# Weight splits behind the reading of each attention projection, and group 0's scaling taken out of the merge

## The chip, the core and the metric

The kernel runs on one core of a Trainium2 chip. The metric is the device time of one execution in microseconds (us). Engines are named as in the profile: PE (matmuls), PEld (its weight loads), DVE (vector), ACT (scalar), POOL (GpSimd) and SP (which only issues DMAs here).

## The reference, cut to what matters

One inference step of a two-layer decoder for 512 prompt positions and 8 sample sequences of 8 positions, all in float32. Layer 0 mixes positions by attention and a pooling mixer, layer 1 by a short convolution; a gated feed-forward half-step stands before and behind each mixer. The attention has 8 heads and three dilation groups, whose outputs are merged with weights from their softmax denominators:

```python
for g, (win, dil) in enumerate(DIL_PATTERNS):      # (128,1), (512,4), (2048,16)
    q, k, v = qk[:, :, g, 0], qk[:, :, g, 1], qkv[:, :, g, 2]     # q, k after rotary
    ...
    o, lse = dilated_attn_prompt(q, k, v, dil)     # or dilated_attn_sample with the cache
    outs.append(o); lses.append(lse)
wts = jax.nn.softmax(jnp.stack(lses, axis=0), axis=0)[..., None]
a = jnp.sum(wts * jnp.stack(outs, axis=0), axis=0)
```

## The kernel before

All 576 tokens lie on the free axis. Each float32 product is made of three matmuls with rounded parts: a weight unit comes by one DMA of 1 MB into `raw` (two buffers), and each half of it is split into a high part `wh` (an ACT cast) and the rest `wl` (a DVE subtraction), line 100 and 101, with three buffers of each. `Weights.next(ahead)` first emits the splits up to `ahead` halves beyond the one that is used now. The split of a unit's second half is followed at once by the DMA of the unit after next into the freed `raw` buffer, on SP's queue, which also carries the loads of the cached keys and values.

The attention loop (lines 1081 to 1114) runs over four pairs of heads. For each it makes six projections (48 matmuls each): q and k of group 1, of group 2 and of group 0. Between the projections stands the rest of the work of the pair of heads before: scores of group 0 (P0), the sample scores, the merge, the transposes of the scaled probabilities and the products with the values. The order is written out by hand and kept: each engine takes its instructions in program order. What sets the pace beside that is PSUM: projections, scores, transposes and products share four buffers named `acc`, used in turn, so each new one waits until the one four places earlier has been read.

`rotate` makes a projection and reads it on DVE: a product with the rotary table (line 1291) and a shuffle (line 1292). POOL then multiplies the shuffled copy (line 1293) and forms q (lines 1311 and 1312) or k (lines 1322 and 1325). `merge` works out the group weights (`mw`, ending in line 1396) and scales the probabilities: P1 on ACT (line 1403), P2 on DVE (line 1405), the first half of P0 on DVE (line 1409) and the second on POOL (lines 1411 and 1414). `sample_weights` (lines 1504 to 1508) scales the sample probabilities on DVE; `sample_pv` ends in the copy `So` out of PSUM (line 1536); `transposes` (line 1427) end in copies `PT` (lines 1430 and 1434). After the loop the last pair's rest stands among four projections for the pooling mixer, which call `proj` directly.

Of the kernel before, what the change touches and what calls it, by code (L numbers as in the profile page):

```python
# [34 lines left out]
KD = 8  # L35
# [132 lines left out]
def ch(t):  # L168

    return t.rearrange("p (c n) -> p c n", c=2)  # L170


class Trunk:
# [216 lines left out]
        self.turn(outs, f, toks)  # L390


    def part(self, p, rh, rl, k0, kn, first, last, mid={}):
        nc = self.nc
        h, l = self.W.next()
        for k in range(kn):
            wh = h[:, k * 128:k * 128 + 128]
            wl = l[:, k * 128:k * 128 + 128]
            for z, (w, m) in enumerate(((wh, rh), (wh, rl), (wl, rh))):
                for c in range(2):  # L400
                    nc.tensor.matmul(out=p[:, c, :C], lhsT=w, rhs=m[:, k0 + k, c * C:c * C + C],  # L401
                                     start=(first and k == 0 and z == 0), stop=(last and k == kn - 1 and z == 2))
            if k in mid:
                mid[k]()

    def proj(self, rh, rl, mid={}):
        p = self.acc()
        self.part(p, rh, rl, 0, KD, True, True, mid)
        return p


# [617 lines left out]
class Mixer:  # L1029
# [5 lines left out]
    def run(self, nxt, u0):  # L1035
        t, nc, I = self.t, self.nc, self.I
        with ExitStack() as ctx:
# [42 lines left out]
            prev = None  # L1080
            for hp in range(4):
                cur = {"hp": hp, "U": self.tile("U", [128, 2, 3, 2, 8], bufs=2), "ks": self.tile("ks", [128, 4, 64], bufs=2),
                       "q": {}, "k": {}, "P": {}, "PT": {}, "qbd": self.qbd[hp % 2], "S": {}, "N": {}, "ST": {}, "SN": {}, "so": {}}
                self.q(cur, 1)
                if prev:
                    self.scores0(prev)
                    self.sample_scores(prev, 0)
                    self.exchange(prev)
                    self.sample_weights(prev, 0)
                self.k(cur, 1)  # L1090
                if prev:
                    self.sample_transposes(prev, 0)
                    self.sample_scores(prev, 1)
                    self.merge(prev)
                    self.sample_weights(prev, 1)
                self.q(cur, 2)
                if prev:
                    self.sample_pv(prev, 0)
                    self.transposes(prev, (1, 2, (0, 0)))
                self.scores12(cur, 1)  # L1100
                self.k(cur, 2)
                if prev:
                    self.pv(prev)
                    self.sample_transposes(prev, 1)
                    self.sample_out(prev, 0)
                self.q(cur, 0)
                self.scores12(cur, 2)
                if prev:
                    self.sample_pv(prev, 1)
                self.k(cur, 0)  # L1110
                if prev:
                    self.sample_out(prev, 1)
                self.new_keys(cur, 0)
                prev = cur
# [8 lines left out]
            self.sample_transposes(prev, 0)  # L1123
            self.sample_scores(prev, 1)
            self.merge(prev)
            self.sample_weights(prev, 1)
            self.pool_in(pu, 2)
            self.pool_diff(3)
# [37 lines left out]
            for e, d in enumerate(ORDER):  # L1166
                p = t.proj(t.xh, t.xl)
# [116 lines left out]

    def rotate(self):
        t, nc = self.t, self.nc
        p = t.proj(t.xh, t.xl)
        self.flush()
        a = self.tile("rot", [128, 720], bufs=4)[:, :NT]
        b = self.tile("rot", [128, 720], bufs=4)[:, :NT]  # L1290
        nc.vector.tensor_tensor(out=ch(a), in0=p[:, :, :C], in1=ch(self.rope[:, 0, :]), op=ALU.mult)
        nc.vector.stream_shuffle(ch(b), p[:, :, :C], SWAP16)
        nc.gpsimd.tensor_tensor(out=b, in0=b, in1=self.rope[:, 1, :], op=ALU.mult)
        return a, b

# [48 lines left out]
    def scores12(self, s, g):  # L1344
        nc, t = self.nc, self.t
        p = t.acc()
        P = s["P"][g] = self.tile(f"P{g}", [128, 2, 4, 128])
        for h in range(2):
# [3 lines left out]
        for h in range(2):  # L1352
            for r in range(4):
                self.softmax_rows(s, g, 2 * r + h, p[:, h, 128 * r:128 * r + 128], self.m1 if g == 1 else self.m2, P[:, h, r, :])

    def scores0(self, s):
        nc, t = self.nc, self.t
        P = s["P"][0] = self.tile("P0", [128, 2, 4, 256])
        for h in range(2):
# [6 lines left out]
            for i in range(4):  # L1366
                lo = 128 if i == 0 else 0
                self.softmax_rows(s, 0, 2 * i + h, p[:, i // 2, (i % 2) * 256 + lo:(i % 2) * 256 + 256], self.m0[:, lo:], P[:, h, i, lo:])

# [9 lines left out]
    def merge(self, s):  # L1379

        nc, U = self.nc, s["U"]
        m = self.tile("mm", [128, 2, 8])
        e = self.tile("me", [128, 2, 3, 8])
        d = self.tile("md", [128, 2, 8])
        w = self.tile("mw", [128, 2, 3, 8])
        tt = nc.vector.tensor_tensor
        over_g = lambda v: v.unsqueeze(2).to_broadcast([128, 2, 3, 8])
        tt(out=m, in0=U[:, :, 0, 0], in1=U[:, :, 1, 0], op=ALU.min)
        tt(out=m, in0=m, in1=U[:, :, 2, 0], op=ALU.min)
        tt(out=e, in0=over_g(m), in1=U[:, :, :, 0], op=ALU.subtract)  # L1390
        nc.scalar.activation(out=e, in_=e, func=AF.Exp)
        tt(out=w, in0=e, in1=U[:, :, :, 1], op=ALU.mult)
        tt(out=d, in0=w[:, :, 0], in1=w[:, :, 1], op=ALU.add)
        tt(out=d, in0=d, in1=w[:, :, 2], op=ALU.add)
        nc.vector.reciprocal(out=d, in_=d)
        tt(out=w, in0=e, in1=over_g(d), op=ALU.mult)
        for g in (1, 2):
            for h in range(2):
                for r in range(4):
                    x = s["P"][g][:, h, r, :]  # L1400
                    col = w[:, 0, g, 2 * r + h:2 * r + h + 1]
                    if g == 1:
                        nc.scalar.activation(out=x, in_=x, func=AF.Copy, scale=col)
                    else:
                        nc.vector.tensor_scalar(out=x, in0=x, scalar1=col, scalar2=None, op0=ALU.mult)
        P = s["P"][0]
        for i in range(4):
            x = P[:, 0, i, 128:] if i == 0 else P[:, 0, i, :]
            nc.vector.tensor_scalar(out=x, in0=x, scalar1=w[:, 1, 0, 2 * i:2 * i + 1], scalar2=None, op0=ALU.mult)
        x = P[:, 1, 0, 128:]  # L1410
        nc.gpsimd.tensor_tensor(out=x, in0=x, in1=w[:, 1, 0, 1:2].to_broadcast([128, 128]), op=ALU.mult)
        x = P[:, 1, 1:4, :]
        wb = w[:, 1, 0].rearrange("p (i h) -> p h i", h=2)[:, 1, 1:4].unsqueeze(2).to_broadcast([128, 3, 256])
        nc.gpsimd.tensor_tensor(out=x, in0=x, in1=wb, op=ALU.mult)
# [332 lines left out]
```

## Time and profile before

| | |
|---|---|
| runs of the kernel | 2281.59, 2284.46, 2287.17 us; median 2284.46 us |
| profiled execution | 2283.84 us, of which the instructions span 2282.1 us |
| PE busy | 2215.2 us (97%) |
| DVE busy | 1623.6 us (71%) |
| ACT busy, POOL busy | 926.3 us (41%), 444.2 us (19%) |
| mean granted TensorE clock | 0.989 |

The numbers in the rows further down are microseconds from the first instruction of the profiled execution. A row of the timeline merges equal instructions that follow each other on one engine; the first column is its start, the second the time that it covers, and a bracket gives the idle time of the engine before it and what ended that. An instruction that has been issued but stands still counts as running, so a long row can hold waiting. Busy shares are averages: what matters for this change is the stretch of the attention loop, where the rows are read one by one.

### The profile page before, as it was taken

To read this page: it belongs to the slowest core of one execution; us is meant where nothing else is said; L and a number is where in the kernel's file an instruction comes from. 1 tells how busy PE (TensorE), PEld (TensorE's weight loads), DVE (VectorE), ACT (ScalarE), POOL (GpSimd) and SP (SyncE) were. 2 spreads that over 40 slices of the span, in tenths; PEclk is the share of its full clock that TensorE was granted. 3 is DMA by queue.
4 is the path that set the end of the run, shared out by engine and by line. 5 is a ranking of instruction groups with operands and counts; after the bars stand their busy time and mean duration, and the time that the engine had idled before them with its cause. 6 is when DMAs were issued, how large, how long until landed. Compare 5 with 4: busy or idle time off the path is not lost.

```text
span 2282.1 us, 39849 instructions
## 1 busy us (share of the span) xinstructions
PE 2215.2 (97%) x16544; PEld 2165.3 (95%) x16544; DVE 1623.6 (71%) x2606; ACT 926.3 (41%) x1611; POOL 444.2 (19%) x443
## 2 busy tenths in 40 slices
PE   8899999999999998999999899999999999999998
PEld 7899999899888898999999899999999999999998
DVE  7687787525666788678697867869554577868783
ACT  5343444323333335344354534435421245435353
POOL 0010111307555641010012101001222111001012
PEclk9999999999999999999999999999999999999999
DMA  4223222443443422322222222322222212322222
GB/s 136 73 81 103 87 93 84 150 152 105 130 140 106 136 96 68 98 91 90 90 91 86 67 91 84 105 90 92 86 94 74 84 66 72 104 84 82 95 99 64
DMA packets 70949, 217.89 MB, mean 95 GB/s; under 512 B 14256, under 2 KB 37808, under 8 KB 54128
## 3 DMA queue, kind: packets, MB, share of 16 engines
q1 hardware_dynamic: 70336, 215.24, 28.4%
q8 instruction: 130, 2.13, 0.4%
q14 instruction: 51, 0.42, 0.1%
q10 hardware_dynamic: 432, 0.10, 0.0%
HBM read 204.22 MB, written 11.10 MB: 94 GB/s over the span
## 4 chain that ended last, share of the span: by engine, by line
PE 50%; DVE 10%; ACT 2%; issue 2%; POOL 0%; POOLq 0%; ACTq 0%; DVEq 0%
PE B L420 11%; PE acc L401 11%; PE F L706 8%; PE A L706 8%; PE F L420 6%; PE A L420 6%; DVE wl L101 2%; DVE sum L112 1%; DVE sum L111 1%; ACT wh L100 1%; DVE dl L101 1%; DVE sum L113 1%; DVE h L445 0%; DVE h L427 0%; ACT dh L100 0%
## 5 line engine op out<-in xcount | busy, mean ns | idle before, releaser
L101 DVE TENSOR_TENSOR wl<-raw,wh 128x1024 fp32r<-128x1024 f32 (+3 forms) x305 | 338.8, 1115 | 195.1 <-ACT wh L100 173.8
L100 ACT CAST wh<-raw 128x1024 fp32r<-128x1024 f32 (+3 forms) x305 | 278.6, 916 | 327.2 <-PE F L706 200.7
L447 POOL TENSOR_TENSOR hl<-h,hh 128x576 fp32r<-128x576 f32 x88 | 138.8, 1577 | 1323.2 <-ACT hh L446 1323.2
L101 DVE TENSOR_TENSOR wl<-sum,wh 128x1024 fp32r<-128x1024 f32 x168 | 204.8, 1225 | 21.9 <-ACT wh L100 21.9
L100 ACT CAST wh<-sum 128x1024 fp32r<-128x1024 f32 x168 | 173.8, 1048 | 106.9 <-DVE sum L112 106.2
L420 PE MATMUL B<-xh,wh 128*128 128x288 f32 x680 | 203.7, 300 | 8.6 <-ACT u L581 4.5
L420 PE MATMUL A<-exh,wh 128*128 128x288 f32 x680 | 203.6, 299 | 6.0 <-ACT B L539 5.7
L401 PE MATMUL acc<-xh,wh 128*128 128x288 f32 x960 | 207.8, 298 | 0.5 <-DVE x L794 0.5
L420 PE MATMUL A<-exh,wl 128*128 128x288 f32 x680 | 202.1, 297 | 4.2 <-DVE wl L101 4.2
L401 PE MATMUL acc<-xl,wh 128*128 128x288 f32 x960 | 205.7, 296 | 0.4 <-POOL xl L1597 0.4
L401 PE MATMUL acc<-xh,wl 128*128 128x288 f32 x960 | 205.5, 296 | 0.0
L706 PE MATMUL F<-hh,wh 128*128 128x288 f32 x690 | 205.0, 297 | 0.0
L706 PE MATMUL F<-hh,wl 128*128 128x288 f32 x690 | 204.8, 297 | 0.0
L420 PE MATMUL B<-xl,wh 128*128 128x288 f32 x680 | 203.3, 299 | 1.6 <-DVE xl L315 1.5
L706 PE MATMUL F<-hl,wh 128*128 128x288 f32 x690 | 204.7, 297 | 0.0
L706 PE MATMUL A<-hl,wh 128*128 128x288 f32 x690 | 203.3, 295 | 0.0
L706 PE MATMUL A<-hh,wh 128*128 128x288 f32 x690 | 203.2, 295 | 0.0
L706 PE MATMUL A<-hh,wl 128*128 128x288 f32 x690 | 203.2, 294 | 0.0
L420 PE MATMUL B<-xh,wl 128*128 128x288 f32 x680 | 202.9, 298 | 0.0
L420 PE MATMUL A<-exl,wh 128*128 128x288 f32 x680 | 201.9, 297 | 0.0
L401 PEld LDWEIGHTS acc<-xh,wh 128*128 128x128 f32 x960 | 154.2, 189 | 4.9 <-issue 2.0
L401 PEld LDWEIGHTS acc<-xl,wh 128*128 128x128 f32 x960 | 154.6, 189 | 0.7 <-POOL xl L1597 0.6
(385 smaller groups left out, 5999.9 us busy)
## 6 DMA issues: line engine op xcount, KB each, us to landing
raw<-in_gu SPq DMA_DIRECT2D x87, 1024.0 KB, 4.9
raw<-in_dn SPq DMA_DIRECT2D x48, 640.0 KB, 3.8
raw<-in_dn SPq DMA_DIRECT2D x16, 896.0 KB, 4.5
raw<-in_wqk SPq DMA_DIRECT2D x12, 1024.0 KB, 4.8
raw<-in_cv SPq DMA_DIRECT2D x12, 1024.0 KB, 4.8
kv<-in_kb SPq DMA_DIRECT2D x32, 256.0 KB, 4.0
kv<-in_vb SPq DMA_DIRECT2D x32, 256.0 KB, 4.7
raw<-in_wv SPq DMA_DIRECT2D x6, 1024.0 KB, 4.8
```

What stands on the lines that cost most here:

```text
L100: self.nc.scalar.copy(out=h, in_=src)
L101: self.nc.vector.tensor_tensor(out=l, in0=src, in1=h.bitcast(F32), op=ALU.subtract)
L111: tt(out=b[:, 0:2], in0=r[:, 0:4:2], in1=r[:, 2:4], op=ALU.add)
L112: tt(out=b[:, 2], in0=b[:, 1], in1=r[:, 0], op=ALU.add)
L113: tt(out=b[:, 3], in0=b[:, 2], in1=r[:, 1], op=ALU.add)
L401: nc.tensor.matmul(out=p[:, c, :C], lhsT=w, rhs=m[:, k0 + k, c * C:c * C + C], start=(first and k == 0 and z == 0), stop=(last and k == kn ...
L420: nc.tensor.matmul(out=out, lhsT=a[:, v], rhs=m, start=(first and k == 0 and z == 0), stop=(last and k == 3 and z == 2), skip_group_check= ...
L447: nc.gpsimd.tensor_tensor(out=self.hl[:, j, :], in0=s["h"], in1=self.hh[:, j, :].bitcast(F32), op=ALU.subtract)
L706: nc.tensor.matmul(out=p[c][:, :C], lhsT=a, rhs=m[:, k, c * C:c * C + C], start=(k == 0 and z == 0), stop=(k == kc - 1 and z == 2))
```

## The change

It has three parts. First, `rotate` asks only for the splits up to one half ahead before its matmuls, and emits the split of the second half ahead after the projection has been read by lines 1291 and 1292. Second, the scaling of P0 is taken out of `merge` into a function `merge0`, which in the loop stands, with the second sample scaling, behind the projection `q(cur, 2)`; after the loop it follows `merge` as before. Third, in the loop the transposes of P0's first half stand behind the scores of group 1 and no longer ahead of them.

```diff
-    def part(self, p, rh, rl, k0, kn, first, last, mid={}):
+    def part(self, p, rh, rl, k0, kn, first, last, mid={}, ahead=2):
...
-        h, l = self.W.next()
+        h, l = self.W.next(ahead)
...
                     self.sample_scores(prev, 1)
                     self.merge(prev)
-                    self.sample_weights(prev, 1)
                 self.q(cur, 2)
                 if prev:
+                    self.merge0(prev)
+                    self.sample_weights(prev, 1)
                     self.sample_pv(prev, 0)
-                    self.transposes(prev, (1, 2, (0, 0)))
+                    self.transposes(prev, (1, 2))
                 self.scores12(cur, 1)
+                if prev:
+                    self.transposes(prev, ((0, 0),))
                 self.k(cur, 2)
...
             self.merge(prev)
+            self.merge0(prev)
             self.sample_weights(prev, 1)
...
     def rotate(self):
-        p = t.proj(t.xh, t.xl)
+        p = t.proj(t.xh, t.xl, ahead=1)
...
         nc.vector.stream_shuffle(ch(b), p[:, :, :C], SWAP16)
+        t.W.ahead(1)
         nc.gpsimd.tensor_tensor(out=b, in0=b, in1=self.rope[:, 1, :], op=ALU.mult)
```

In the changed kernel lines below `rotate` have higher numbers: 1291 and 1292 became 1295 and 1296; 1293, 1311, 1312, 1322 and 1325 became 1298, 1316, 1317, 1327 and 1330; 1341 became 1346; 1405, 1409, 1411 and 1414 became 1411, 1418, 1420 and 1423; 1504 to 1508 became 1513 to 1517; 1536 became 1545.

The first place is DVE at the start of a loop pass with a pair of heads before it: the reading of k of group 0, the reading of the next pair's q of group 1, and the first scores of P0 (here `P_5509`). Before:

```order
L101 TENSOR_TENSOR wl<-raw,wh 128x1024
L1291 TENSOR_TENSOR rot<-acc,rope 128x576
L1292 STREAM_SHUFFLE rot<-acc 128x576
L101 TENSOR_TENSOR wl<-raw,wh 128x1024
L1291 TENSOR_TENSOR rot<-acc,rope 128x576
L1292 STREAM_SHUFFLE rot<-acc 128x576
L1341 ISA P_5509,U<-acc,cst 128x128
```

And in the changed kernel:

```order
L1295 TENSOR_TENSOR rot<-acc,rope 128x576
L1296 STREAM_SHUFFLE rot<-acc 128x576
L101 TENSOR_TENSOR wl<-raw,wh 128x1024
L1295 TENSOR_TENSOR rot<-acc,rope 128x576
L1296 STREAM_SHUFFLE rot<-acc 128x576
L101 TENSOR_TENSOR wl<-raw,wh 128x1024
L1346 ISA P_5509,U<-acc,cst 128x128
```

The split that stood ahead of the second reading stands behind it, ahead of the scores.

The second place is DVE behind the merge of the same pass; `P_5351` is P2, `P_5509` is P0, the reading is that of q of group 2. Before:

```order
L1405 TENSOR_SCALAR P_5351<-P_5351,mw 128x128 x8
L1409 TENSOR_SCALAR P_5509<-P_5509,mw 128x128
L1409 TENSOR_SCALAR P_5509<-P_5509,mw 128x256 x3
L1504 RECIPROCAL Sst<-Sst 128x1
L1507 TENSOR_SCALAR N<-S,Sst 128x32
L1508 TENSOR_SCALAR S<-S,Sst 128x4x128
L101 TENSOR_TENSOR wl<-raw,wh 128x1024
L1291 TENSOR_TENSOR rot<-acc,rope 128x576
L1292 STREAM_SHUFFLE rot<-acc 128x576
L1536 COPY So<-acc 128x128
```

And in the changed kernel:

```order
L1411 TENSOR_SCALAR P_5351<-P_5351,mw 128x128 x8
L1295 TENSOR_TENSOR rot<-acc,rope 128x576
L1296 STREAM_SHUFFLE rot<-acc 128x576
L101 TENSOR_TENSOR wl<-raw,wh 128x1024
L1418 TENSOR_SCALAR P_5509<-P_5509,mw 128x128
L1418 TENSOR_SCALAR P_5509<-P_5509,mw 128x256 x3
L1513 RECIPROCAL Sst<-Sst 128x1
L1516 TENSOR_SCALAR N<-S,Sst 128x32
L1517 TENSOR_SCALAR S<-S,Sst 128x4x128
L1545 COPY So<-acc 128x128
```

The reading of q went up to stand right behind P2; the split, P0's four products and the sample scaling now stand between that reading and the copy `So`.

The third place is POOL in the same stretch: P0's second half and the forming of q of group 2. Before:

```order
L1411 TENSOR_TENSOR P_5509<-P_5509,mw 128x128
L1414 TENSOR_TENSOR P_5509<-P_5509,mw 128x768
L1293 TENSOR_TENSOR rot<-rot,rope 128x576
L1311 TENSOR_TENSOR mxa<-rot 64x512
L1312 TENSOR_TENSOR qbd_4504<-rot 64x8x8
L1311 TENSOR_TENSOR mxa<-rot 64x512
L1312 TENSOR_TENSOR qbd_4504<-rot 64x8x8
```

And in the changed kernel:

```order
L1298 TENSOR_TENSOR rot<-rot,rope 128x576
L1316 TENSOR_TENSOR mxa<-rot 64x512
L1317 TENSOR_TENSOR qbd_4504<-rot 64x8x8
L1316 TENSOR_TENSOR mxa<-rot 64x512
L1317 TENSOR_TENSOR qbd_4504<-rot 64x8x8
L1420 TENSOR_TENSOR P_5509<-P_5509,mw 128x128
L1423 TENSOR_TENSOR P_5509<-P_5509,mw 128x768
```

The two products of P0 went from ahead of the forming of q to behind it.

## Rows read from the trace of the kernel before

**Rows 1.** Stretches: us, busy time of each engine, granted clock, DMA share, GB/s.

```profile
560.00:600.00 40.00, 36.31 (x352) 32.90 (x351) 29.65 (x93) 17.59 (x55) 25.65 (x38) 0.96 0.42 136
690.00:732.00 42.00, 37.89 (x366) 34.71 (x365) 30.33 (x98) 19.38 (x57) 26.67 (x39) 0.96 0.40 130
```

**Rows 2.** Waits of PE, 508 to 805 us: line, awaited line, total, times, longest.

```profile
PE acc L1427 <- DVE rot L1292: 9.3, 3, 3.7
...
PE acc L1533 <- DMA kv<-in_vb: 2.0, 3, 1.1
```

**Rows 3.** Timeline of PE, second loop pass (the first row: the first pass).

```profile
528.47 2.05 PE L1350 MATMUL acc<-kt,mxa 128*128 128x128 f32 x16 [0.90 <-POOL kt L1322]
...
578.15 1.06 PE L1533 MATMUL acc<-kv,PT 128*32 128x128 f32 x26 [0.28 <-DMA kv<-in_vb]
...
579.50 1.97 PE L1427 MATMUL acc<-ident,P 128*128 128x128 f32 x16
584.42 1.13 PE L1427 MATMUL acc<-ident,P 128*128 128x128 f32 x7 [2.96 <-DVE rot L1292]
585.34 3.45 PE L1350 MATMUL acc<-kt,mxb 128*128 128x128 f32 x16
```

**Rows 4.** Timeline of DVE, second loop pass.

```profile
553.43 1.20 DVE L101 TENSOR_TENSOR wl<-raw,wh 128x1024 fp32r<-128x1024 f32 x1
558.06 0.76 DVE L1291 TENSOR_TENSOR rot<-acc,rope 128x576 f32<-128x576 f32 x1 [3.43 <-POOL kv L1480]
...
568.88 1.22 DVE L101 TENSOR_TENSOR wl<-raw,wh 128x1024 fp32r<-128x1024 f32 x1
...
576.90 3.13 DVE L1405 TENSOR_SCALAR P<-P,mw 128x128 f32<-128x128 f32 x8
579.95 1.06 DVE L1409 TENSOR_SCALAR P<-P,mw 128x128 f32<-128x128 f32 x4
...
581.67 1.22 DVE L101 TENSOR_TENSOR wl<-raw,wh 128x1024 fp32r<-128x1024 f32 x1
582.81 0.75 DVE L1291 TENSOR_TENSOR rot<-acc,rope 128x576 f32<-128x576 f32 x1
...
584.17 0.28 DVE L1536 COPY So<-acc 128x128 f32<-128x128 f32 x1
```

**Rows 5.** Timeline of POOL, second loop pass.

```profile
576.94 0.40 POOL L1411 TENSOR_TENSOR P<-P,mw 128x128 f32<-128x128 f32 x1 [1.10 <-DVE mw L1396]
577.30 1.47 POOL L1414 TENSOR_TENSOR P<-P,mw 128x768 f32<-128x768 f32 x1
584.36 1.42 POOL L1293 TENSOR_TENSOR rot<-rot,rope 128x576 f32<-128x576 f32 x1 [5.58 <-DVE rot L1292]
585.85 2.10 POOL L1311 TENSOR_TENSOR mxa<-rot 64x512 f32<-64x512 f32 x1
587.92 0.31 POOL L1312 TENSOR_TENSOR qbd<-rot 64x64 f32<-64x64 f32 x1
588.29 2.15 POOL L1311 TENSOR_TENSOR mxa<-rot 64x512 f32<-64x512 f32 x1
590.38 0.34 POOL L1312 TENSOR_TENSOR qbd<-rot 64x64 f32<-64x64 f32 x1
```

**Rows 6.** Single lines, 508 to 770 us: shortest, median, longest of one, in ns.

```profile
L1405 DVE TENSOR_SCALAR P<-P,mw x24: 274/276/1508, 576.9 to 710.0; 128x128 f32<-128x128 f32 x24
...
L1377 DVE COPY U<-U x64: 159/167/2004, 562.9 to 761.1; 32x8 f32<-32x8 f32 x64
...
L1293 POOL TENSOR_TENSOR rot<-rot,rope x24: 1406/1416/2243, 516.7 to 748.6; 128x576 f32<-128x576 f32 x24
```

**Rows 7.** Timeline of SP, second loop pass.

```profile
570.12 0.33 SPq L74 DMA_DIRECT2D raw<-in_wqk  x1
570.95 2.11 SPq L1474 DMA_DIRECT2D kv<-in_vb  x3
```

**Rows 8.** A short stretch of the second pass, columns as in rows 1.

```profile
586.00:588.00 2.00, 2.00 (x11) 2.00 (x11) 0.56 (x1) 0.23 (x1) 2.00 (x2) 0.50 0.00 0
```

More of the change, by code (lines that the diff above doesn't have):

```diff
@@ L404, in part, with proj @@
                 mid[k]()
-    def proj(self, rh, rl, mid={}):
+    def proj(self, rh, rl, mid={}, ahead=2):
         p = self.acc()
-        self.part(p, rh, rl, 0, KD, True, True, mid)
+        self.part(p, rh, rl, 0, KD, True, True, mid, ahead)
         return p
@@ L1396, in merge @@
         tt(out=w, in0=e, in1=over_g(d), op=ALU.mult)
+        s["mw"] = w
         for g in (1, 2):
@@ L1405, in merge, with merge0 @@
                         nc.vector.tensor_scalar(out=x, in0=x, scalar1=col, scalar2=None, op0=ALU.mult)
-        P = s["P"][0]
+    def merge0(self, s):
+        nc, w, P = self.nc, s["mw"], s["P"][0]
         for i in range(4):
```

## The prediction

> **What bounds the kernel now.** I read the page's busy shares first: PE is the engine that is never far from full, and time can be won or lost only where PE stands. Then the stretches of the attention loop: in two of the three passes shown, PE is busy for 36.31 of 40.00 us and for 37.89 of 42.00 us, at a mean granted clock of 0.96 [rows 1]; the stretches between are full. So some 4 us of each of the three later passes are idle, all in one place, and that bounds what this change can give back. The view of waits names it: three times, 9.3 us together, a transpose of line 1427 stood until DVE had read a projection (line 1292) [rows 2]. The timelines of the second pass show why [rows 3, 4]. The transposes of P1 and P2 run from 579.50 to 581.47; those of P0 need the `acc` buffer of q of group 2, which DVE reads only from 582.81 on, because P2's and P0's scaling, the sample scaling and a split stand ahead of it. PE idles 2.96 us and then works at half clock: the granted clock is 0.50 at 586 to 588 us [rows 8], the lower of the two levels (1.2 and 2.4 GHz), and the scores of group 1 take 3.45 us where the same 16 took 2.05 us in the first pass [rows 3]. The next projection begins at 585.34 + 3.45 = 588.79. The passes repeat after 65.1 us (the 24 products of line 1405 run from 576.9 to 710.0), so one pass is worked out and taken three times.
>
> **The port that DVE and POOL share.** Three rows decide this forecast [rows 6]. A P2 product takes 276 ns, but one in each pass 1508 ns: it stands while POOL's 1.47 us product of P0 runs (577.30 to 578.77) [rows 5]. A copy of line 1377, 167 ns, once takes 2004 ns beside a POOL operation; and POOL's line 1293, 1.42 us, takes up to 2.24 us where it starts into a split of DVE. So operations of the two engines with all operands in SBUF exclude each other for their whole length, and whichever runs makes the other stand. Readings of PSUM are not seen to suffer.
>
> **The change part by part.**
>
> *Splits behind the reading.* The same number of splits, 1.20 to 1.22 us each. The one that ran at 553.43, in front of 3.43 us of DVE idle time [rows 4], goes behind the reading that ended that idle time, into a stretch in which DVE is nearly always busy down to `So`. That delays the merge by 0 (if another wait absorbs it) to 1.2 us; I take 1.0, near the upper end. PE's transposes of the sample scores, its products and the transposes of P1 and P2 shift with it. The split at 568.88 goes behind a reading of 584.17 - 582.81 = 1.36 us and so ends at 568.88 + 1.0 + 1.36 + 1.22 = 572.5. SP's load of the next weights starts when that split ends (570.12 against 568.88 + 1.22 = 570.10), and the cached values queued behind it at 570.95 [rows 7] then start near 572.8, 1.9 us later. PE already waits for them until 578.15 [rows 3]: 580.05 now, the transposes of P1 and P2 begin at 579.50 + 1.9 = 581.4 and end at 583.4, and the scores of group 1 behind them end at 585.4. The splits themselves are not late: a whole projection of 48 matmuls stands between each split and its use. For the first pass and the four projections after the loop I count nothing; a split's 1.2 us bounds that to either side.
>
> *P0's scaling behind the reading of q.* P2 now begins at 576.90 + 1.0 = 577.9 and is no longer held by POOL's product of P0: 3.13 - (1.508 - 0.276) = 1.90 us, so 579.8. The reading ends at 581.2, 3 us before its old 584.17. The wait of 9.3 us is thus really gone: the buffer is free before the transposes of P1 and P2 are over. What is late next is P0. Its transposes need the four products of line 1409, and the buffer of the sample products, freed by `So`, which stands on DVE behind the split, those four products and three operations of sample scaling: 1.22 + (581.67 - 579.95 = 1.72) us without hindrance [rows 4]. But the same reading releases POOL's forming of q: line 1293, then 1311, 1312, 1311, 1312, and now P0's second half behind them, 1.42 + 2.10 + 0.31 + 2.15 + 0.34 + 0.40 + 1.47 = 8.19 us [rows 5]. Before, POOL did this while DVE read PSUM; now it meets seven DVE operations in SBUF. P2 got one product through between POOL's two products of P0, so I let DVE pass one operation for each of POOL's: seven for seven. `So` begins at 581.2 + 1.22 + 8.19 + 0.5 = 591.1 (0.5 for what of DVE's own 1.72 us is not covered; an estimate between 0 and 1.7). No hindrance at all is one end, 584.1; 591.1 + 1.2 the other.
>
> *Transposes of P0 behind the scores.* The scores fill the old gap, a gain of up to 2.96 us, but PE then stands from 585.4 to 591.1 + 0.28 + 0.1 = 591.5, takes 585.34 - 584.42 = 0.92 us for the transposes, and begins the next projection at 592.4: 3.6 us later than before. The clock: an idle time of 2.96 us cost 3.45 - 2.05 = 1.4 us, which stands in the old 588.79 already; now the idle time is some 6 us and the low clock falls on the transposes and the next projection. Between 0 and 1.4 us more; I take 0.6. POOL's second half of P0 is needed only behind the next projection, and the later copies `PT` on ACT delay nobody sooner.
>
> Sum: 3.6 + 0.6 = 4.2 us in each of three passes, 12.6 us. Behind each pass PE is full again, so nothing is given back. The profiled execution took 2283.84 us, 0.6 us under the median of the runs: 2283.84 + 12.6 + 0.6 = 2297 us.
>
> **The rivals.**
>
> *Two operations in each gap of POOL.* DVE issues its next product before the last has ended; if two get through at a time, the seven are done with POOL's fourth operation: 1.42 + 2.10 + 0.31 + 2.15 = 5.98 instead of 8.19 us. `So` begins at 588.9, the projection at 590.2: 1.4 us late, 2.0 with the clock, 6 us in all, 2290 us. For it: POOL's operations that wait for one another start with small gaps. Against it: the one P2 product of rows 6.
>
> *DVE keeps the port (faster).* If DVE, once it has run the split, holds the port through P0's products, and POOL stands instead, `So` begins at 581.2 + 1.22 + 1.72 = 584.1 and the transposes follow the scores without a gap, 585.4 + 0.92 = 586.3: 2.5 us earlier than 588.79, 7.5 us in all, 2277 us. It decides from the point where P0's products are issued ahead of POOL's next operation each time. Against it: line 1377's 2004 ns, a DVE copy in a row of 16 that POOL overtook. The Trainium skill (SBUF — State Buffer, Who interferes with whom) counts tensor_scalar among the operations that can take the shared pair, and says that whoever issues first has it for the whole instruction while the other blocks. The 1508 ns agree with the blocking; by the issue order alone, a DVE that is always first would give this rival's time.
>
> *The wait only changes its place.* `So` comes near 588, so that the projection starts where it did: 2284 us, within 4 us. It needs POOL's chain to be half hidden, which no row shows.
>
> *More than forecast.* The longer idle time costs the clock twice, and the merge moves by 1.2 us more: 6 us a pass, 2302 us.
>
> **How the numbers follow.** One for one 0.53, two in a gap 0.18, DVE keeps the port 0.15, the wait moves 0.08, more 0.06. The prediction is the first, 2297 us, its own range 2290 to 2302. What a measurement of this kernel can tell from no change is about 0.2%, 4.6 us. Faster takes the port rival: 0.16. Within 0.2%: the moved wait and a third of the two-in-a-gap case, 0.14. Slower: the rest, 0.70. The range leaves out the port rival and the last few of the highest: 2282 to 2303 us.
>
> **What would show it.** In the profile after: no wait of line 1427 for the reading of a projection, but three of some 5 to 6 us for `So` (or for P0's products); P2's eight products in 1.9 us; P0's four products in 5 us or more, single ones over 2000 ns; the group of lines that forms q begun earlier, at about 581.3; PE's next projection 3 to 5 us later in each pass; values of the cache 2 us later. I am wrong if P0's products stay near 1.1 us together (then the port rival holds), or if the low clock is gone from the passes.

## The result and the profile after

| | before | changed |
|---|---|---|
| median of the runs | 2285.51 us (4 runs, 2281.59 to 2287.17) | 2300.24 us (4 runs, 2298.99 to 2300.55) |
| profiled execution | 2283.84 us | 2300.33 us |
| PE busy | 2215.2 us | 2219.3 us |

The changed kernel is slower: the ratio is 1.0064, with an interval of 1.0051 to 1.0076, 14.7 us by the medians. The forecast was 2297 us, 12.6 us more than before.

The first view is the page of the changed kernel: its span, and busy time, share and instructions of each engine.

```profile
span 2298.5 us, 39840 instructions
...
PE 2219.3 (97%) x16544; PEld 2167.9 (94%) x16544; DVE 1627.4 (71%) x2606; ACT 924.3 (40%) x1611; POOL 451.3 (20%) x443
```

Shares hide the change, so the loop is cut out: one stretch from the first to the last of the 24 POOL products behind a projection's reading (columns as in [rows 1]). Of the kernel before:

```profile
516.70:748.60 231.90, 219.47 (x1970) 207.04 (x1969) 147.24 (x439) 88.07 (x263) 146.42 (x176) 0.98 0.37 121
```

And of the changed kernel, with the stretch that answers to the first of [rows 1] and one of two microseconds behind the new wait:

```profile
517.50:762.40 244.90, 222.10 (x1970) 208.47 (x1970) 151.43 (x438) 87.69 (x263) 153.38 (x176) 0.97 0.34 112
...
560.00:600.00 40.00, 32.51 (x279) 29.57 (x278) 33.26 (x93) 16.36 (x52) 24.61 (x36) 0.91 0.32 110
...
592.00:594.00 2.00, 2.00 (x10) 2.00 (x10) 1.92 (x17) 1.47 (x7) 0.00 (x0) 0.50 0.00 0
```

The loop is 13.0 us longer. The same 1970 matmuls are busy 2.6 us longer, which is the clock; the other 10.4 us are idle PE. The waits of PE say for what (stretch of the loop; line, awaited line, total, times, longest). Before, beside the 9.3 us of [rows 2]:

```profile
PE acc L1515 <- DVE S L1508: 1.4, 3, 0.5
PE acc L1533 <- DMA kv<-in_vb: 0.9, 2, 0.6
```

After:

```profile
PE acc L1436 <- DVE So L1545: 15.8, 3, 5.7
PE acc L1524 <- DVE S L1517: 4.1, 3, 1.4
PE acc L1542 <- DMA kv<-in_vb: 2.0, 5, 0.5
```

The wait for the reading of a projection is gone. In its place stand three waits for `So`, 5.3 us each on average. The scaled sample probabilities cost 2.7 us more, the cached values 1.1 us.

The second pass shows how, and is the counterpart of [rows 3 to 5]. PE:

```profile
580.29 1.06 PE L1542 MATMUL acc<-kv,PT 128*32 128x128 f32 x26 [0.44 <-DMA kv<-in_vb]
...
583.43 1.95 PE L1355 MATMUL acc<-kt,mxb 128*128 128x128 f32 x16
591.10 1.75 PE L1436 MATMUL acc<-ident,P 128*128 128x128 f32 x7 [5.71 <-DVE So L1545]
```

DVE:

```profile
573.94 0.57 DVE L1393 TENSOR_TENSOR mm<-U 128x16 f32<-128x16 f32 x1
574.54 0.18 DVE L1394 TENSOR_TENSOR mm<-mm,U 128x16 f32<-128x16 f32 x1
...
578.31 1.66 DVE L1411 TENSOR_SCALAR P<-P,mw 128x128 f32<-128x128 f32 x8
579.88 0.75 DVE L1295 TENSOR_TENSOR rot<-acc,rope 128x576 f32<-128x576 f32 x1
...
581.74 2.20 DVE L101 TENSOR_TENSOR wl<-raw,wh 128x1024 fp32r<-128x1024 f32 x1 [0.37 <-ACT wh L100]
583.86 4.95 DVE L1418 TENSOR_SCALAR P<-P,mw 128x128 f32<-128x128 f32 x4
588.73 0.15 DVE L1513 RECIPROCAL Sst<-Sst 128x1 f32<-128x1 f32 x1
588.91 0.26 DVE L1516 TENSOR_SCALAR N<-S,Sst 128x32 f32<-128x32 f32 x1
589.08 1.75 DVE L1517 TENSOR_SCALAR S<-S,Sst 128x512 f32<-128x512 f32 x1
590.76 0.28 DVE L1545 COPY So<-acc 128x128 f32<-128x128 f32 x1
```

POOL:

```profile
574.55 2.14 POOL L1327 TENSOR_TENSOR kt<-rot 128x512 f32<-128x512 f32 x1
...
581.45 1.41 POOL L1298 TENSOR_TENSOR rot<-rot,rope 128x576 f32<-128x576 f32 x1 [4.19 <-DVE rot L1296]
582.93 2.96 POOL L1316 TENSOR_TENSOR mxa<-rot 64x512 f32<-64x512 f32 x1
585.86 0.31 POOL L1317 TENSOR_TENSOR qbd<-rot 64x64 f32<-64x64 f32 x1
586.23 2.10 POOL L1316 TENSOR_TENSOR mxa<-rot 64x512 f32<-64x512 f32 x1
588.29 0.37 POOL L1317 TENSOR_TENSOR qbd<-rot 64x64 f32<-64x64 f32 x1
588.73 0.40 POOL L1420 TENSOR_TENSOR P<-P,mw 128x128 f32<-128x128 f32 x1
589.09 1.47 POOL L1423 TENSOR_TENSOR P<-P,mw 128x768 f32<-128x768 f32 x1
```

The two lists are to be read side by side; their rows ahead of 578 us belong to the merge and are taken up with the rivals below. The split waits 0.37 us for ACT's cast `wh`, is issued at 581.74, while POOL's first product runs, and takes 2.20 us where 1.22 us is its length: it ends 1.1 us behind that product. POOL's second operation, issued at 582.93 into the split, takes 2.96 us where 2.10 is its length. P0's four products, 1.06 us together before [rows 4], take 4.95 us, and the last scaling, 0.48 us elsewhere, ends behind POOL's last operation: 589.09 + 1.47 = 590.56, and `So` starts at 590.76. Each DVE operation in SBUF got through behind one of POOL's: seven behind seven. The reciprocal of one column (0.15 us) is not seen to wait.

Last, SP, which answers to [rows 7]:

```profile
573.22 0.33 SPq L74 DMA_DIRECT2D raw<-in_wqk  x1
```

### The profile page after: what moved, and what is told of

The parts are those of the page before. It is cut to its first block, busy times and chain, and to the rows that moved or that the text cites. A ratio compares the mean times of both kernels' runs of the same rounds, so it can differ in the third digit from the quotient of the medians.

```text
span 2298.5 us, 39840 instructions
## 1 busy us (share of the span) xinstructions
PE 2219.3 (97%) x16544; PEld 2167.9 (94%) x16544; DVE 1627.4 (71%) x2606; ACT 924.3 (40%) x1611; POOL 451.3 (20%) x443
## 4 chain that ended last, share of the span: by engine, by line
PE 51%; DVE 9%; ACT 2%; issue 2%; POOL 0%; POOLq 0%; ACTq 0%; DVEq 0%
PE B L420 11%; PE acc L401 11%; PE F L706 8%; PE A L706 8%; PE F L420 7%; PE A L420 6%; DVE wl L101 2%; DVE sum L112 1%; DVE sum L111 1%; ACT wh L100 1%; DVE dl L101 0%; DVE sum L113 0%; DVE h L445 0%; DVE h L427 0%; DVE xl L315 0%
## 5 line engine op out<-in xcount | busy, mean ns | idle before, releaser
L101 DVE TENSOR_TENSOR wl<-raw,wh 128x1024 fp32r<-128x1024 f32 (+3 forms) x305 | 334.0, 1099 | 173.4 <-ACT wh L100 152.2
```

The costliest lines, as they stand in the source:

```text
L101: self.nc.vector.tensor_tensor(out=l, in0=src, in1=h.bitcast(F32), op=ALU.subtract)
```

## The experiments

All seven kernels were timed beside the kernel before, whose medians there were 2285.37 us (for the first three below and P0 on ACT) and 2285.87 us (for the other three). Theory A is the prediction's: one operation of DVE for each of POOL's, behind the reading of q of group 2. Rival B blames the later splits, rival C the longer line of work on DVE ahead of `So`, whatever POOL does.

### Part 1 alone: the splits behind the readings

```diff
-        p = t.proj(t.xh, t.xl)
+        p = t.proj(t.xh, t.xl, ahead=1)
...
+        t.W.ahead(1)
```

(on the kernel before, with the argument handed through as in the change)

> The kernel before with the first part of the change alone: the splits stand behind the reading of each projection, P0's scaling and the transposes stand where they were. Theory A (the shared port: seven DVE operations in SBUF wait one for one for POOL's seven behind the reading of q of group 2): here P0's four products and the sample scaling run ahead of that reading, so POOL's chain meets the split alone, which costs at most one wait of 1.4 us; the reading comes 0.6 us sooner (merge 0.55 us later, split of 1.2 us gone from ahead of it), the copy So 1 to 2 us later. Per pass -0.6 to +1.2 us, in all 2284 to 2290 us against 2285.5 before. Theory B (the later splits and the DMAs behind them are what costs): all of the loss is here, 2300 us.

Measured: 2283.24 us, ratio 0.9991 (0.9983 to 1.0000), just under the expected range. The later splits are not what costs. PE in the second pass, and the loop:

```profile
585.96 0.95 PE L1428 MATMUL acc<-ident,P 128*128 128x128 f32 x7 [0.77 <-DVE rot L1292]
587.26 2.02 PE L1351 MATMUL acc<-kt,mxb 128*128 128x128 f32 x16 [0.35 <-DVE So L1537]
```

```profile
518.80:746.00 227.20, 217.03 (x1970) 202.81 (x1969) 136.98 (x438) 88.05 (x263) 153.40 (x176) 1.00 0.37 121
```

The old gap of 2.96 us [rows 3] is cut to 0.77 and 0.35 us, since the split no longer stands ahead of the reading, and the 16 scores take 2.02 us instead of 3.45: the low clock is gone from the loop, whose PE is busy 2.4 us less. Against that, PE's waits for the scaled sample probabilities rise from 2.4 to 4.8 us (508 to 825 us). By the loop it is 4.7 us shorter, by the medians 2.1 us. The rest of this execution took longer than that of the kernel before, 2.1 us ahead of the loop and 1.9 us behind it. Over all nine traces the loop starts between 516.0 and 518.8 us, though nothing ahead of it differs, so 1 or 2 us between two single executions say little.

### Parts 2 and 3 alone: the scaling and the transposes, splits as before

```diff
-                    self.sample_weights(prev, 1)
                 self.q(cur, 2)
                 if prev:
+                    self.merge0(prev)
+                    self.sample_weights(prev, 1)
...
-                    self.transposes(prev, (1, 2, (0, 0)))
+                    self.transposes(prev, (1, 2))
                 self.scores12(cur, 1)
+                if prev:
+                    self.transposes(prev, ((0, 0),))
```

> The change without its first part: the splits stand ahead of each projection as in the kernel before, P0's scaling and the second sample scaling behind the reading of q of group 2, P0's transposes behind the scores. Theory A (the shared port): P2 ends near 578.5, the split near 579.7, the reading near 581, then P0's products meet POOL's chain of 8.2 us, So near 589.8 and the next projection 2.5 us late plus up to 1.4 us of low clock in each of three passes: 2294 to 2299 us, a wait of some 5 us for So in each pass. Theory B (the later splits cost): 2285 us, as before.

Measured: 2300.46 us, ratio 1.0061 (1.0049 to 1.0073): the whole loss of the change, and a little above the expected range. DVE in the second pass:

```profile
584.89 4.24 DVE L1417 TENSOR_SCALAR P<-P,mw 128x128 f32<-128x128 f32 x4
...
589.24 1.94 DVE L1515 TENSOR_SCALAR N<-S,Sst 128x32 f32<-128x32 f32 x1
...
591.62 0.28 DVE L1544 COPY So<-acc 128x128 f32<-128x128 f32 x1
```

With the split ahead of the reading, DVE has six operations left, of which the first is issued ahead of POOL's (584.89 against 585.07), so five pass behind five of POOL's, and the stall falls on others: `N`, 0.26 us in the changed kernel, takes 1.94. The loop takes 244.1 us, against 244.9. Not all of it is that meeting: the split waits 1.76 us for ACT's cast and holds up the reading of q, and the scores of group 1 wait 3.1 us in the loop for that reading, beside 14.4 us for `So`. What part 1 saves alone, it does not save beside parts 2 and 3.

### POOL's forming of q of group 2 left out

```diff
-        for h in range(2):
+        for h in range(0 if g == 2 and s["hp"] > 0 else 2):
```

(on the changed kernel; passes 2 to 4 then use a q of group 2 that was not formed)

> The changed kernel with four POOL operations left out: the forming of q of group 2 (lines 1316 and 1317) in the second to fourth loop pass, so that q of group 2 there is not what the reference computes; DVE's work and order are unchanged. Theory A (the shared port): POOL's chain behind the reading shrinks by 2.10 + 0.31 + 2.10 + 0.37 = 4.9 us, So comes 4 to 5 us sooner (586 to 587 instead of 590.8 in the second pass), 2285 to 2289 us, and the longest of P0's products falls from 2.2 us to at most 1.5 us. Theory C (DVE's own queue ahead of So is what is long, whatever POOL does): 2300 us and P0's products as long as in the changed kernel.

Measured: 2282.89 us, ratio 0.9988 (0.9979 to 0.9997), 2 us better than the range of theory A, although `So` came a little later than expected (587.56) and the longest of P0's products took 1.57 us, not at most 1.5. DVE, then PE, in the second pass:

```profile
584.47 2.44 DVE L1418 TENSOR_SCALAR P<-P,mw 128x128 f32<-128x128 f32 x4
...
587.17 0.48 DVE L1517 TENSOR_SCALAR S<-S,Sst 128x512 f32<-128x512 f32 x1
587.56 0.28 DVE L1545 COPY So<-acc 128x128 f32<-128x128 f32 x1
```

```profile
587.90 0.98 PE L1436 MATMUL acc<-ident,P 128*128 128x128 f32 x7 [2.00 <-DVE So L1545]
```

The order on DVE is untouched, and four of POOL's seven operations are gone. P0's products fall from 4.95 to 2.44 us and PE's wait from 5.71 to 2.00 us. This refutes rival C. In the loop PE idles 11.3 us less than in the changed kernel; the rest of the gain, 5.7 us less busy PE, is the clock, which the expectation had left out: behind 2.00 us of idle time the seven transposes take 0.98 us, not 1.75.

### POOL's forming done twice

```diff
-        for h in range(2):
+        for h in (0, 1, 0, 1) if g == 2 and s["hp"] > 0 else (0, 1):
```

> The changed kernel with POOL's forming of q of group 2 done twice over in the second to fourth loop pass (lines 1316 and 1317, the same result written again): 4.9 us more for POOL ahead of P0's second half. Theory A1 (one for one: each DVE operation in SBUF waits for one POOL operation at most): P0's four products get through behind the first forming as before, the sample scaling then waits for 2.1 and 0.3 us where it waited for 0.4 and 1.5 us, So about 0.5 to 2.5 us later: 2302 to 2309 us. Theory A2 (DVE gets through only when POOL's chain is over): So 4.9 us later in each of three passes, 2315 us. Theory C (DVE's own queue): 2300 us.

Measured: 2302.51 us, ratio 1.0072 (1.0059 to 1.0086). The time rules out that DVE gets through only when POOL's chain is over (2315 us), but hardly tells theory A from rival C; the trace does. DVE, then POOL, in the second pass:

```profile
581.13 0.75 DVE L1295 TENSOR_TENSOR rot<-acc,rope 128x576 f32<-128x576 f32 x1
...
585.12 4.97 DVE L1418 TENSOR_SCALAR P<-P,mw 128x128 f32<-128x128 f32 x4
...
590.19 1.95 DVE L1516 TENSOR_SCALAR N<-S,Sst 128x32 f32<-128x32 f32 x1
...
592.59 0.28 DVE L1545 COPY So<-acc 128x128 f32<-128x128 f32 x1
```

```profile
592.46 2.20 POOL L1316 TENSOR_TENSOR mxa<-rot 64x512 f32<-64x512 f32 x1
594.62 0.31 POOL L1317 TENSOR_TENSOR qbd<-rot 64x64 f32<-64x64 f32 x1
```

DVE does not wait for POOL's longer queue: `So` comes at 592.59, with one long forming operation, a short one and P0's second half still to end on POOL. It starts 11.46 us behind the start of the reading, against 590.76 - 579.88 = 10.88 in the changed kernel. One for one asks for just this: the last two of the seven that DVE passes are now 2.09 and 0.31 us long instead of 0.40 and 1.47, 0.53 us more.

### The old place of P0's transposes

```diff
-                    self.transposes(prev, (1, 2))
+                    self.transposes(prev, (1, 2, (0, 0)))
                 self.scores12(cur, 1)
-                if prev:
-                    self.transposes(prev, ((0, 0),))
```

> The changed kernel without its third part: P0's transposes ahead of the scores of group 1 again. Theory A (the wait is for P0's products and So, behind the port): the transposes wait for P0's fourth product near 588.8, the scores then for So near 591.0, and the next projection comes 0.5 to 1.5 us later in each pass: 2300 to 2305 us. If the place of the transposes were what costs, it would be 2286 us.

Measured: 2304.78 us, ratio 1.0083 (1.0070 to 1.0097). Waits of PE, 508 to 825 us:

```profile
PE acc L1434 <- DVE P L1416: 10.7, 6, 2.4
...
PE acc L1353 <- DVE So L1543: 5.0, 3, 1.9
```

The transposes now wait for P0's products one by one, and the scores behind them for `So`. So part 3 is a gain in itself, 4.5 us, once part 2 has made P0 late. Most of it is the clock: in the loop PE idles only 0.4 us more here than in the changed kernel, but is busy 4.1 us longer with the same matmuls (226.2 against 222.1 us, at a granted clock of 0.95 against 0.97).

### P0's first half on ACT, the sample scaling ahead of the reading

```diff
+                    self.sample_weights(prev, 1)
                 self.q(cur, 2)
                 if prev:
-                    self.merge0(prev)
-                    self.sample_weights(prev, 1)
+                    self.merge0(prev, True)
...
+                nc.scalar.activation(out=x, in_=x, func=AF.Copy, scale=w[:, 1, 0, 2 * i:2 * i + 1])
```

(on the changed kernel; `True` takes the ACT form)

> The changed kernel with P0's first half scaled on ACT in the loop and the second sample scaling back ahead of q of group 2: behind the reading DVE has only the split in SBUF. Theory A (the shared port): So near 583.5 in the second pass, the transposes of P0 follow the scores of group 1 at about 585.4 without a wait of more than 0.5 us, the next projection 3.3 us sooner than in the kernel before in each of three passes: 2275 us. Theory C (DVE's queue ahead of So, whatever POOL does): the four products and the sample scaling gone from it shorten it by 1.7 us, so So near 589 and 2295 us.

Measured: 2277.86 us, ratio 0.9968 (0.9957 to 0.9980), 2.9 us above the expected time. In the second pass, DVE, PE and ACT:

```profile
581.59 0.28 DVE L1548 COPY So<-acc 128x128 f32<-128x128 f32 x1
```

```profile
581.93 1.95 PE L1355 MATMUL acc<-kt,mxb 128*128 128x128 f32 x16
583.72 0.93 PE L1439 MATMUL acc<-ident,P 128*128 128x128 f32 x7
```

```profile
580.07 1.60 ACT L1419 ACTIVATE P<-P,mw 128x128 f32<-128x128 f32 x4
```

With nothing left for DVE to do in SBUF beside POOL but the split, `So` starts 1.0 us behind the end of the reading, and PE has no gap here. The split ran in its usual 1.21 us, as it was issued (580.47) ahead of POOL's first product (580.65), which stood in turn.

### A version that beats both

The bad meeting has a second remedy: leave P0's first half and the sample scaling ahead of the reading, as before the change, and move only POOL's half of P0 behind the forming of q. DVE's P2 and P0 products then find POOL idle. The split that stood ahead of this one reading goes behind the copies `PT`.

```diff
-                self.q(cur, 2)
+                self.q(cur, 2, 1 if prev else 2)
                 if prev:
+                    self.merge1(prev)
                     self.sample_pv(prev, 0)
                     self.transposes(prev, (1, 2, (0, 0)))
+                    t.W.ahead(1)
```

(on the kernel before; `merge1` holds POOL's two products of P0, and `q` hands the number to `proj`)

> From the kernel before: P0's first half and the second sample scaling stay ahead of the reading of q of group 2; POOL's half of P0 goes behind the forming of that q, and of the splits only the one at that projection is put off, behind So and the copies PT. Theory A (the shared port): P2 takes 1.7 us instead of 3.1 us since POOL is idle beside it, the split's 1.2 us is gone from ahead of the reading, which so ends near 581.6 instead of 584.2, when the transposes of P1 and P2 end: no wait, no low clock, the next projection 3.5 to 4.3 us sooner in each of three passes: 2272 to 2275 us. If it is DVE's work in all that counts, whatever its neighbour on POOL: 1.2 us a pass, 2282 us.

Measured: 2273.89 us (2272.27 to 2274.30), ratio 0.9948 (0.9936 to 0.9961), 12 us under the kernel before and 26 under the changed one. DVE, PE and the loop:

```profile
577.78 1.66 DVE L1408 TENSOR_SCALAR P<-P,mw 128x128 f32<-128x128 f32 x8
579.36 1.07 DVE L1412 TENSOR_SCALAR P<-P,mw 128x128 f32<-128x128 f32 x4
...
581.08 0.75 DVE L1294 TENSOR_TENSOR rot<-acc,rope 128x576 f32<-128x576 f32 x1
```

```profile
582.70 0.96 PE L1434 MATMUL acc<-ident,P 128*128 128x128 f32 x7 [0.54 <-DVE rot L1295]
```

```profile
517.60:736.70 219.10, 214.71 (x1970) 202.18 (x1969) 145.00 (x439) 87.98 (x263) 149.27 (x175) 1.00 0.40 127
```

P2 and P0 run unhindered, the gap shrinks from 2.96 to 0.54 us, the clock stays high, and the loop is 12.8 us shorter than before: 8.0 us less idle PE and 4.8 us less busy PE for the same matmuls. POOL's half of P0 and the split were not moved one at a time, so what each is worth alone is not shown.

## Why the prediction was right, step by step

**What goes.** The wait of 9.3 us went, as said. The reading of q began at 579.88 and released POOL at 581.45; the forecast had its end at 581.2.

**What comes in its place.** The forecast let DVE pass one operation for each of POOL's, from one row of P2 held for 1508 ns [rows 6]. The trace after shows that exchange seven times in each pass, and the two experiments on POOL's forming, less and more, move `So` as it asks. The count of seven is in part luck. The forecast put the split ahead of the chain and let the reciprocal take a turn; in the trace the split, late by its wait for ACT, takes the first turn, and the reciprocal takes none. The split so cost 0.9 us (POOL's 2.96 - 2.10) and not 1.22, and the 0.5 us put on for DVE's own time was a little too much, as 0.20 us lay between POOL's end and `So`. `So` was forecast for 591.1 and came at 590.76. As the loop of this execution starts 0.8 us later (517.50 against 516.70), it came some 1.1 us sooner within the pass than forecast. The wait, some 6 us in the forecast, is 5.71 here and 5.3 on average.

**The rivals.** "Two in a gap" would have freed `So` at 588.9: no. "DVE keeps the port" would have left P0's products near 1.1 us: they took 4.95. The Trainium skill (SBUF — State Buffer, Who interferes with whom) says that whoever issues first has the shared pair for the whole instruction and the other blocks; the rows agree, 2.20 us for a split issued into POOL's product and 2.96 us for POOL's operation issued into that split. What the rows add is what follows between two engines that both have the next operation ready: the split, P0's products and the sample scaling take turns with POOL's operations, and in no pass of the changed kernel do two of them get through behind one. It is no rule for every operation. In the merge (first rows of the two lists above) two of DVE's operations on 128x16 get through between a POOL operation that ends at 574.48 and the next at 574.55, the second at its usual 0.18 us; copies of line 1382 (1377 before), 0.16 us each, do the same, one held until POOL's operation ends at 565.30 and another at 565.34, just ahead of POOL's next at 565.35. So the rival's two in a gap does occur, with shorter operations than those of this change, and the row of line 1377 that the forecast set against another rival holds an example of it.

**The splits.** The merge was forecast 1.0 us later. P2 starts at 578.31 against 576.90, 1.4 us later, of which 0.8 us is the later start of the loop. PE's waits for the scaled sample probabilities rose by 4.1 - 1.4 = 2.7 us in the loop, 0.9 per pass. The load of the weights was forecast for 572.5 and started at 573.22, and PE's values of the cache came at 580.29 against 580.05 in the forecast, both with the same 0.8 us in them. Part 1 alone also took the low clock out of the kernel before, a gain that the forecast did not price; beside parts 2 and 3 nothing of it is left to see.

**P2.** Forecast 1.90 us, measured 1.66: none of the eight is held.

**The clock and the waits** are two terms that were both mis-sized, by about as much and in opposite directions, and this is why the total came so close. The 3.6 us a pass of the forecast hold 1.9 us of later work ahead of P0's transposes, 6.1 - 2.96 = 3.1 us of longer wait behind the scores, and 1.4 us less for the scores, which run at the high level again. That is 5.0 us more idle PE a pass, 15.1 in all; with the 0.6 us of clock it is 0.8 us less busy PE a pass, 2.4 in all. Measured are 10.4 us more idle PE (6.5 by the waits for `So`, 15.8 against the 9.3 of the old wait, and 3.8 by the two waits ahead of them) and 2.6 us more busy PE. The waits were forecast 4.7 us too long in the three passes, and the clock's price 5.0 us too small. In the second pass the low level (1.2 GHz, a granted clock of 0.50) covers the transposes, 1.75 us where 0.92 was counted, and the next projection until about 596.5 us: the granted clock is 0.50 at 594 to 596 us, 0.76 at 596 to 598 us and 1.00 behind that.

**The sum.** In the loop, 12.6 us forecast and 13.0 measured, a hit of the mechanism and of the direction, but in its closeness luck. The rest of the 14.7 us lies outside. The two profiled executions differ by 16.4 us of span, 3.4 more than the loop: 0.8 us ahead of it, where nothing was changed, and 2.6 us behind it, for which the forecast counted nothing. Of these, 1.1 us is PE's wait for `So` of the last pair of heads (2.1 against 1.0 us); the other 1.5 us stays open. The profiled execution before lay 1.7 us under the median of its four runs (2285.51 us), while the one after lies at its own, so the scatter of single executions may be enough for it.

## What to carry to other kernels

Before an elementwise step is moved behind a reading, look at what the same reading releases on POOL: two engines that meet in SBUF take turns, and a chain of short DVE operations then runs at the pace of POOL's long ones. Moving the other side of the meeting (POOL's half of P0) or giving the work to ACT keeps the gain of an earlier or unhindered reading without the price. Look for one operation in a group whose longest time is several times its median; it is the cheapest sign of such a meeting, and here it told where the new wait would be.

## What was not expected of the hardware

The exchange between DVE and POOL is strict for the operations of this change: with four of POOL's operations gone, P0's products take 2.44 us; with them, 4.95; with four more, 4.97. Work on ACT is not held: its eight products of P1 took 2.45 us in the kernel before, beside POOL's two products of P0 (both from 576.9 us on), and 2.46 us in the changed one, with POOL idle (from 578.31). P0's four products on ACT took 1.60 us, 0.40 each, but say less, as POOL's operation beside them stood behind the split for most of that time.

The clock did not fall at every gap. Behind 2.00 us of idle time (no forming) the transposes ran at the high level, 0.98 us; behind 2.96 us [rows 3] and 5.71 us work followed at the low one. In the faster version, with gaps of at most 1.0 us here, the granted clock of the whole loop was 1.00, and 4.8 us of its gain are that.
